# Softmax times V on one core: who writes an identity matrix, and sixteen words sent early

## The chip, the core and the metric

The kernel runs on one core of a Trainium2 chip. The core has five engines that run their own instruction streams and meet through semaphores: TensorE (PE in the profile, with its weight loads as PEld), VectorE (DVE), ScalarE (ACT), GpSimd (POOL) and SyncE (SP), which here only issues DMAs. 16 DMA engines move data between DRAM and the on-chip memory SBUF; PSUM holds what TensorE writes. The metric is the device time of one execution in microseconds (us), as the median of several. The profile shows one execution in detail.

## The reference

```python
scores: (8, 12, 1024, 1024) float32      v: (8, 12, 1024, 64) float32
scores_max = np.max(scores, axis=-1, keepdims=True)
attn = np.exp(scores - scores_max)
attn = attn / (np.sum(attn, axis=-1, keepdims=True) + 1e-8)
return np.matmul(attn, v).astype(np.float32)
```

96 heads, and for each a 1024 x 1024 matrix of scores whose rows become weights, and a product with a 1024 x 64 matrix. The scores are 403 MB, v and the result 25 MB each.

## The kernel before

**Tiling.** A pass takes four heads, as two groups `k` of two heads each; there are 24 passes, counted by `m` from 0 to 23 in one loop. In a group, a partition holds 16 rows of scores of one head (64 partitions for each head), so `s_nat` of a group is 128 x 16 x 1024 values, 8 MB. There is one such buffer for each group.

**One row.** Below, a row `r` of a group means the 128 score rows, one for each partition, that have the same place. For every two rows ScalarE writes the exponentials in half precision into one of six `p_nat` buffers (line 461). TensorE turns each row in eight blocks against the identity `ident16` into PSUM, `psT` (line 474); VectorE copies two turned rows into `pt` (line 486, the last four rows of group 1 one by one on line 482); TensorE multiplies `pt` by `vones`, v with columns of ones beside it, and sums into `psO` (line 172). The products of a row follow its transposes three rows later. For every three rows VectorE takes the reciprocals of the sums (line 150) and writes the normalised result into `out_sb`, in two halves (line 158). The maximum isn't subtracted; VectorE keeps the extremes of the reciprocals and a last check on them (lines 353 to 374) decides whether `general()`, a slow way that subtracts the maximum, runs behind the loop. With these inputs it does not.

**Order on the queues.** All transfers are issued by SyncE, in an order that `queue()` fixes. Within a pass m, when group 0 is done (`load_first`), SyncE issues v of the next pass, a store of the results of the pass before, and group 0's scores of the next pass; when group 1 is done (`last`), group 1's scores. GpSimd spreads v into `vones` (line 321) and moves `out_sb` into `done` (line 202), from which the store of a whole pass goes out in one DMA (line 226). That store carries a condition: in pass 0 there is nothing to store, and in pass 22 it is left out. The results of passes 21 and 22 go out in pass 23 from `done` and from `v_sb` (line 237, in `load_first`), and those of pass 23 in three pieces from `out_sb` (line 237, in `end`).

**The last passes.** From pass 21 on, the loads for the next pass are cut into pieces (group 0: 8, 4 and 4 rows; group 1: 4, 4, 2, 2, 2, 1 and 1), in the `Else` of two conditions. In the first 22 passes `ident16` is a permuted identity (line 82), which puts two neighbouring rows of the result into neighbouring partitions as `done` needs them; passes 22 and 23 store straight from `out_sb` and need the plain one. So in `last`, in the `Else` that passes 21 and 22 take, line 442 writes `ident16` anew, from `ident32`; that writing must wait until TensorE has turned the last row of the pass, and TensorE's next transposes wait for it. On ScalarE it stands behind `watch_v` (line 335), which reads all of v, and in front of the next pass's exponentials; the loop has no barrier, each engine goes on into the next pass as its semaphores allow.

**Declared orders.** `apart(a, b)` tells the planner that two instructions need no order between them; `send()` does this for all stores and keeps them in `stores`.

Of the kernel before, what the change touches and what calls it, by code (L numbers as in the profile page):

```python
# [26 lines left out]
def kernel(  # L27
# [6 lines left out]
    nc = tc.nc  # L34
# [5 lines left out]
    BH = B * H  # L40
# [12 lines left out]
    T = 2  # L53
    K = AHEAD // T
    W = P // T
# [12 lines left out]
    out_rows = out.rearrange("b h (j r) d -> (b h j) (r d)", j=W)  # L68
# [8 lines left out]
    ident32 = const_pool.tile([P, P], FP32, name="ident32")  # L77
    make_identity(nc, ident32)
    ident16 = const_pool.tile([P, P], FP16, name="ident16")
# [3 lines left out]
        out=ident16[:].rearrange("x (t a j) -> x t a j", t=T, a=A),  # L83
        in_=ident32[:].rearrange("x (t j a) -> x t a j", t=T, a=A),
# [38 lines left out]
    def after(a, b):  # L123

        tc.add_manual_dep(
            a.ins,
            b.ins.name,
            mybir.DependencyInfo(mybir.DependencyClass.NoSync, mybir.DependencyReason.DATA),
            reason="order",
        )  # L130
# [7 lines left out]
    def queue(dma):  # L138

        if queued:  # L140
            after(dma, queued[-1])
        queued.append(dma)
# [43 lines left out]
    def behind(a, b, reason):  # L186

        tc.add_manual_dep(
            a.ins,
            b.ins.name,  # L190
            mybir.DependencyInfo(mybir.DependencyClass.Sync, mybir.DependencyReason.DATA),
            reason=reason,
        )

    def put_by(k):

        first = None
        for t in range(T):
            for a in range(A):
                at = (t * A + a) * J  # L200
                to = (k * T + t) * J
                put = nc.gpsimd.tensor_copy(  # L202
                    out=done[to : to + J, a],
                    in_=out_bufs[k][at : at + J].rearrange("x r d -> x (r d)"),
                )
                fills.append(put)
                first = first or put
        return first

    def put_spare():  # L210

        for k in range(K):
            fills.append(
                nc.gpsimd.tensor_copy(  # L214
                    out=spare[:, k], in_=out_bufs[k][:].rearrange("x r d -> x (r d)")
                )
            )

    def of_pass(m):

        return out_runs[bass.ds(m, 1)].rearrange("o x y -> (o x) y")

    def store_before(m):

        before = (m + (PASSES - 1)) % PASSES
        send(nc.sync.dma_start(out=of_pass(before), in_=runs, cond=(before < PASSES - 3)))

    def send(dma):
        for other in stores:
            apart(dma, other)  # L230
            apart(other, dma)
        apart(dma, dma)
        stores.append(dma)
        queue(dma)

    def store_last(to, rows):
        store = nc.sync.dma_start(out=to, in_=rows)
        ends.append(store)
        send(store)

    def end():

        cut = (GROUPS - 2) * G
        for k, a, b in ((0, 0, R), (1, 0, cut), (1, cut, R)):
            n = BH - AHEAD + T * k
            store_last(
                out_rows[n * W : (n + T) * W, a * D : b * D],
                out_bufs[k][:, a:b, :].rearrange("x r d -> x (r d)"),
            )

    stores, fills, ends, norms = [], [], [], {}
    writers, users = {}, {}

    def apart(a, b, reason="stores of two heads are disjoint"):
        tc.declare_no_dep(a.ins, b.ins, across_iterations=True, reason=reason)
# [18 lines left out]
    def load(k, m, parts=(R,), r=0, **cond):  # L274
        rows_n = sc_rows[bass.ds(m, 1), k].rearrange("o x r k -> (o x) r k")
        for rows in parts:
            queue(
                nc.sync.dma_start(  # L278
                    out=s_bufs[k][:, r : r + rows, :], in_=rows_n[:, r : r + rows, :], **cond
                )  # L280
            )
            r += rows

    def load_first(m, k):


        before = queued[-1:]
        n = (m + 1) % PASSES
        with tc.If(m < PASSES - 1) as cmp:  # L289
            load_v(n)  # L290
            store_before(m)
            then = queued[-1:]
            with tc.If(m < PASSES - 3) as cmp2:
                load(0, n)
            with cmp2.Else():
                queued[:] = then
                load(0, n, (8, 4, 4))
            spread_v(k)
        with cmp.Else():
            queued[:] = before  # L300
            store_last(of_pass(PASSES - 3), runs)
            at = (PASSES - 2) * K * P
            rows = out_rows[at : at + K * P].rearrange("(k x) y -> x k y", x=P)
            store_last(rows, spare)

    def load_v(m, **cond):

        rows = v_bh.rearrange("(m x) y -> m x y", x=P)
        dma = nc.sync.dma_start(
            out=v_sb[:].rearrange("x h s l d -> x (h s l d)"),  # L310
            in_=rows[bass.ds(m, 1)].rearrange("o x y -> (o x) y"),
            **cond,
        )
        fills.append(dma)
        queue(dma)

    def spread_v(k, behind_rows=False):

        for t in range(T):
            for s in range(S):  # L320
                op = nc.gpsimd.tensor_copy(  # L321
                    out=vones[s * Q : (s + 1) * Q, k, :, t, 0:D].rearrange(
                        "i (h l) d -> i h l d", l=L
                    ),
                    in_=v_sb[(k * T + t) * Q : (k * T + t + 1) * Q, :, s],
                )
                if behind_rows and t + s == 0:
                    behind(op, norms[k], "all rows are there")
        return op

    def watch_v():


        junk = p_bufs[-1][:].rearrange("p r k -> p (r k)")
        return nc.scalar.activation(  # L335
            out=junk,
            in_=v_sb[:].rearrange("p h s l d -> p (h s l d)"),
            func=mybir.ActivationFunctionType.Abs,
            scale=1.0 / SUM_MAX,
            accum_out=seen[:, K * R + 1 : K * R + 2],  # L340
        )
# [8 lines left out]
    def fold():  # L350

        n = K * R + 1
        nc.vector.tensor_reduce(out=seen[:, 0:1], in_=seen[:, 0 : n + 1], axis=X, op=ALU.min)  # L353
        nc.vector.tensor_reduce(  # L354
            out=seen[:, n + 1 : n + 2], in_=seen[:, 1 : n + 2], axis=X, op=ALU.max
        )

    def judge(bank):

        n = K * R + 1  # L360
        part = small("part")
        nc.vector.tensor_scalar(
            out=part, in0=seen[:, n + 1 : n + 2], scalar1=1.0, scalar2=None, op0=ALU.is_le
        )
        nc.vector.scalar_tensor_tensor(  # L365
            out=right, in0=seen[:, 0:1], scalar=1.0 / SUM_MAX, in1=part, op0=ALU.is_ge, op1=ALU.mult
        )
        cell = bank[0:1, G * M : G * M + 1]
        in_line(
            nc.tensor.matmul(  # L370
                out=cell, lhsT=right[:], rhs=vones[:, 0, 0, 0, D : D + 1], start=True, stop=True
            )
        )
        nc.vector.tensor_copy(out=count[:], in_=cell)
# [45 lines left out]
    def last(m, bank):  # L420

        before = queued[-1:]
        k = K - 1
        with tc.If(m < PASSES - 1) as cmp:
            n = nc.snap(m + 1, min_val=1, max_val=PASSES - 1)
            with tc.If(m < PASSES - 2) as cmp3:
                behind(put_by(0), norms[0], "all rows are there")
                spread_v(k, True)
                watch_v()
                put_by(k)  # L430
            with cmp3.Else():
                spread = spread_v(k)
                watch = watch_v()
                gate = nc.gpsimd.tensor_copy(out=cell, in_=out_bufs[k][:, R - 1, D - 1 : D])
                for op in (watch, spread):
                    behind(gate, op, "the values have been read")
                put_spare()
            with tc.If(m < PASSES - 3) as cmp2:  # L438
                queued[:] = before
                load(k, n)  # L440
            with cmp2.Else():
                nc.scalar.copy(out=ident16[:], in_=ident32[:])  # L442
                queued[:] = before
                load(k, n, (4, 4, 2, 2, 2, 1, 1))
        with cmp.Else():
            queued[:] = before
            end()
            fold()
            judge(bank)
# [96 lines left out]
```

## Time and profile before

| what | time |
|---|---|
| median of 3 runs | 1059.33 us |
| lowest and highest | 1058.65 and 1059.74 us |
| the profiled execution | 1058.67 us |
| its span, first to last instruction | 1056.9 us |
| TensorE and its weight loads busy | 812.7 and 777.8 us |
| ScalarE busy | 750.1 us |
| VectorE busy | 705.1 us |
| GpSimd busy | 418.8 us |

How to read the profile's lines. The page gives a busy line in 40 slices as tenths, queues with packets, MB and share, and groups: line, engine, operation, out <- in, count, then busy us and mean ns of one, then idle time of the engine ahead of it and what released it. A timeline row is: start and duration in us from the span's start, engine, line, operation, out <- in with partitions x elements, count, and in brackets the idle time ahead of it and its releaser. An engine name with a q (SPq) is the engine's sequencer, for instructions that only issue or branch. A row of several instructions gives the time from the first's start to the last's end. A wait for several semaphores is put down to the one that came last by the profile; where the engine named had long been done, it was another. A row of DMA issues ends with the size and the time from issue to landing.

### The profile page before, as it was taken

The page shows a single profiled execution, that of the slowest core. Times are in us where ns is not written, and L with a number is a line of the kernel's source. Part 1 is how long each engine was busy: PE and PEld are TensorE (multiplying, and loading weights), DVE is VectorE, ACT ScalarE, POOL GpSimd, SP SyncE. Part 2 cuts the span into 40 slices and gives each one's busy share as a digit, 9 for nine tenths or more (in the row PEclk, how much of TensorE's full clock was granted, in tenths as well). Part 3 has the DMA queues.
Part 4 walks back from the last instruction along what each step waited for, and adds up shares of the span by engine and source line. Part 5 has one row for each costly group of instructions (what it writes and reads, how often), then busy time and mean ns, then how long its engine had stood idle before and what let it go on. Part 6 is the DMA issues. An engine that isn't in the chain of part 4 may idle for free.

```text
span 1056.9 us, 32833 instructions
## 1 busy us (share of the span) xinstructions
PE 812.7 (77%) x12289; PEld 777.8 (74%) x12289; DVE 705.1 (67%) x1352; ACT 750.1 (71%) x484; POOL 418.8 (40%) x571
## 2 busy tenths in 40 slices
PE   3488668887787867878678877787787876888887
PEld 3487568786787867877668776777777766878787
DVE  2377566676676756677566675676657766667788
ACT  4487578776787667876778667786687856877985
POOL 3063342633525335243362433633336334263340
PEclk9799887898998888899888898898889989789999
DMA  9999999999999999999999999999999999999997
GB/s 397 438 437 424 408 455 422 429 434 427 446 437 437 437 433 438 434 429 434 422 429 434 437 437 437 437 437 416 455 432 432 434 411 440 434 437 424 430 419 322
DMA packets 16692, 453.06 MB, mean 429 GB/s; under 512 B 1840, under 2 KB 1968, under 8 KB 2992
## 3 DMA queue, kind: packets, MB, share of 16 engines
q1 hardware_dynamic: 16688, 452.99, 99.6%
q8 instruction: 4, 0.07, 0.0%
HBM read 427.82 MB, written 27.26 MB: 431 GB/s over the span
## 4 chain that ended last, share of the span: by engine, by line
DMA 61%; PE 13%; ACT 10%; PEld 8%; DVE 5%; issue 1%; POOL 1%; SPq 0%; DVEq 0%; PEldq 0%; ACTq 0%; POOLq 0%
DMA s_nat<-in_scores_dram 61%; ACT p_nat L461 10%; PE psO L172 6%; PE psT L474 6%; PEld L474 4%; DVE pt L486 4%; PEld L172 4%; POOL vones L321 0%; DVE seen L150 0%; DVE out_sb L158 0%; POOL done L202 0%; SPq L278 0%; DVE pt L482 0%; ACTq L461 0%; PEldq L289 0%
## 5 line engine op out<-in xcount | busy, mean ns | idle before, releaser
L461 ACT ACTIVATE p_nat<-s_nat 128x2048 f16<-128x2048 f32 (+1 forms) x432 | 702.4, 1709 | 283.7 <-SPq L438 152.6
L474 PE MATMUL psT<-ident,p_nat 128*128 128x128 f16 x6144 | 517.7, 235 | 209.8 <-ACT p_nat L461 209.8
L486 DVE COPY pt<-psT 128x2048 f16<-128x2048 f16 x336 | 411.2, 1224 | 302.6 <-PE L474 137.2
L474 PEld LDWEIGHTS <-p_nat 128*128 128x128 f16 x6144 | 435.1, 120 | 222.4 <-ACT p_nat L461 222.4
L172 PE MATMUL psO<-vones,pt 128*128 128x130 f16 x6144 | 499.1, 227 | 29.1 <-DVE pt L486 13.2
L321 POOL CAST vones<-v_sb 32x512 f16<-32x512 f32 x384 | 233.2, 607 | 595.2 <-PE L474 316.8
L172 PEld LDWEIGHTS <-pt 128*128 128x128 f16 x6144 | 400.2, 101 | 51.2 <-DVE pt L486 34.0
L158 DVE TENSOR_TENSOR out_sb<-psO,seen 64x192 f32<-64x192 f32 (+1 forms) x576 | 192.0, 333 | 36.9 <-issue 13.0
L202 POOL COPY done<-out_sb 32x1024 f32<-32x1024 f32 x176 | 182.6, 1037 | 10.4
L482 DVE COPY pt<-psT 128x1024 f16<-128x1024 f16 x96 | 63.4, 681 | 1.5
L150 DVE RECIPROCAL seen<-psO 128x3 f32<-128x3 f32 (+1 forms) x288 | 49.4, 172 | 5.1 <-PE L474 1.5
L335 ACT ACTIVATE p_nat<-v_sb 128x2048 f16<-128x2048 f32 x24 | 45.6, 1900 | 0.0
L442 ACT CAST ident<-ident 128x128 f16<-128x128 f32 x2 | 0.6, 298 | 7.7 <-PE psO L172 7.7
L335 ACT ACT_TABLE_LOAD x1 | 1.3, 1283 | 5.8 <-DMA v_sb<-in_v_dram 5.8
L353 DVE TENSOR_REDUCE seen<-seen 128x1 f32<-128x34 f32 x25 | 4.7, 189 | 0.8
L335 ACT ACTIVATION_READ_ACCUMULATOR p_nat<-v_sb 128x1 f32 x24 | 4.5, 188 | 0.0
L354 DVE TENSOR_REDUCE seen<-seen 128x1 f32<-128x34 f32 x25 | 4.5, 179 | 0.0
L108 DVE MEMSET done<- 128x1024 f32 x2 | 1.8, 912 | 1.2 <-DVEq L505 1.0
L214 POOL COPY v_sb<-out_sb 128x1024 f32<-128x1024 f32 x2 | 2.0, 1040 | 0.0
L370 PE MATMUL psO<-vones,right 128*1 128x1 f16 x1 | 0.2, 164 | 1.6 <-DVE right L365 1.6
L370 PEld LDWEIGHTS <-right 128*1 128x1 f16 x1 | 0.1, 79 | 1.8 <-DVE right L365 1.8
masks.py:197 POOL MEMSET ident<- 128x128 f32 x1 | 0.2, 204 | 0.3 <-POOLq L530 0.3
(13 smaller groups left out, 2.0 us busy)
## 6 DMA issues: line engine op xcount, KB each, us to landing
v_sb<-in_v_dram SPq DMA_DIRECT2D x24, 1024.0 KB, 13.5
out_dram<-done SPq DMA_DIRECT2D x24, 1024.0 KB, 8.7
s_nat<-in_scores_dram SPq DMA_DIRECT2D x4, 4096.0 KB, 18.5
s_nat<-in_scores_dram SPq DMA_DIRECT2D x8, 2048.0 KB, 25.9
s_nat<-in_scores_dram SPq DMA_DIRECT2D x6, 1024.0 KB, 29.0
s_nat<-in_scores_dram SPq DMA_DIRECT2D x4, 512.0 KB, 26.8
out_dram<-v_sb SPq DMA_DIRECT2D x1, 1024.0 KB
s_nat<-in_scores_dram SPq DMA_DIRECT2D x43, 28.7
```

The source lines that it names most:

```text
L150: nc.vector.reciprocal(out=recip, in_=psO[:, :, D : D + 1])
L158: norm = nc.vector.tensor_tensor(out=out_bufs[k][part, g * G : g * G + rows, :], in0=psO[part, :, t * N : t * N + D], in1=recip[part].to_b ...
L172: product = nc.tensor.matmul(out=st["psO"][g][:, i * M : (i + 1) * M], lhsT=pt[:, c * P : (c + 1) * P], rhs=vones[:, k, c].rearrange("p t ...
L202: put = nc.gpsimd.tensor_copy(out=done[to : to + J, a], in_=out_bufs[k][at : at + J].rearrange("x r d -> x (r d)"),)
L321: op = nc.gpsimd.tensor_copy(out=vones[s * Q : (s + 1) * Q, k, :, t, 0:D].rearrange("i (h l) d -> i h l d", l=L), in_=v_sb[(k * T + t) * Q ...
L335: return nc.scalar.activation(out=junk, in_=v_sb[:].rearrange("p h s l d -> p (h s l d)"), func=mybir.ActivationFunctionType.Abs, scale=1. ...
L353: nc.vector.tensor_reduce(out=seen[:, 0:1], in_=seen[:, 0 : n + 1], axis=X, op=ALU.min)
L354: nc.vector.tensor_reduce(out=seen[:, n + 1 : n + 2], in_=seen[:, 1 : n + 2], axis=X, op=ALU.max)
L461: exp = nc.scalar.activation(out=p_nat[:, g : g + rows, :].rearrange("p r (x v) -> p x r v", v=Q * L), in_=s_bufs[k][:, r + g : r + g + ro ...
L474: turned = nc.tensor.transpose(out=psT[:, c * P : (c + 1) * P], in_=p_row[:, c // L, c % L, :], identity=ident16[:],)
L482: copy = nc.vector.tensor_copy(out=pt, in_=psT)
L486: copy = nc.vector.tensor_copy(out=pt2[:], in_=psT2[:])
```

## The change

```diff
+    def touch():
+
+        at = (BH - T) * W
+        dma = nc.sync.dma_start(out=out_rows[at : at + 16, 0:1], in_=ident32[0:16, 0:1])
+        for other in stores:
+            apart(dma, other)
+            apart(other, dma)
+        apart(dma, dma)
+        queue(dma)
+
@@ in load_first
             with cmp2.Else():
                 queued[:] = then
                 load(0, n, (8, 4, 4))
+                touch()
             spread_v(k)
@@ in last
             with cmp2.Else():
-                nc.scalar.copy(out=ident16[:], in_=ident32[:])
+                nc.vector.tensor_copy(out=ident16[:], in_=ident32[:])
                 queued[:] = before
                 load(k, n, (4, 4, 2, 2, 2, 1, 1))
```

The first part moves line 442 from ScalarE to VectorE, with the same operands. On VectorE it stands behind the last normalisation of the pass and in front of the next pass's copies.

The second part adds one DMA, issued by SyncE in passes 21 and 22, behind the three loads of group 0. It writes sixteen single words of the result in DRAM, one in each of sixteen partitions' runs, from `ident32`. They lie in the last two heads, whose right values the last stores of pass 23 write over them. The DMA is declared apart from the conditional store and from itself, and it is not in `stores`, so the stores of line 237 are not declared apart from it.

## The prediction

> **What bounds the kernel now.** First the page: busy time, the slices, the queues and the two lines of interest.
>
> ```profile
> span 1056.9 us, 32833 instructions
> ...
> DMA  9999999999999999999999999999999999999997
> ...
> q1 hardware_dynamic: 16688, 452.99, 99.6%
> ...
> L442 ACT CAST ident<-ident 128x128 f16<-128x128 f32 x2 | 0.6, 298 | 7.7 <-PE psO L172 7.7
> ```
>
> The 16 DMA engines move 453 MB and are full in every slice but the last. A change that moves neither bytes nor their order can only act on the last stretch, between the last loads and the end. The second thing is the moved line: two casts of 0.3 us, with 7.7 us of ScalarE idle before them, so 8.3 us of ScalarE time in all. The question is how much of it stands on the path. So next the windows of the last 80 us (columns: busy time of PE, PEld, DVE, ACT, POOL; clock; DMA share; GB/s), and ScalarE's timeline there.
>
> ```profile
> 980.00:1000.00 20.00, 15.64 (x261) 14.85 (x261) 14.13 (x27) 20.00 (x12) 9.02 (x12) 1.00 1.00 425
> ...
> 1020.00:1040.00 20.00, 19.16 (x325) 18.56 (x326) 17.16 (x31) 19.66 (x12) 4.76 (x8) 1.00 1.00 425
> ```
>
> ```profile
> 975.93 0.19 ACT L335 ACTIVATION_READ_ACCUMULATOR p_nat<-v_sb 128x1 f32 x1
> 979.19 0.30 ACT L442 CAST ident<-ident 128x128 f16<-128x128 f32 x1 [3.07 <-PE psO L172]
> 980.00 29.14 ACT L461 ACTIVATE p_nat<-s_nat 128x2048 f16<-128x2048 f32 x18 [0.51 <-PE psO L172]
> ...
> 1010.85 0.19 ACT L335 ACTIVATION_READ_ACCUMULATOR p_nat<-v_sb 128x1 f32 x1
> 1015.62 0.30 ACT L442 CAST ident<-ident 128x128 f16<-128x128 f32 x1 [4.58 <-PE psO L172]
> 1016.43 18.14 ACT L461 ACTIVATE p_nat<-s_nat 128x2048 f16<-128x2048 f32 x10 [0.51 <-PE psO L172]
> 1034.91 10.62 ACT L461 ACTIVATE p_nat<-s_nat 128x2048 f16<-128x2048 f32 x7 [0.34 <-PE psT L474]
> 1046.13 1.06 ACT L461 ACTIVATE p_nat<-s_nat 128x1024 f16<-128x1024 f32 x1 [0.59 <-PE psT L474]
> ```
>
> DMA is full (share 1.00) while ScalarE is busy 20.00 and 19.66 of 20 us and PE 19.16: three resources run level here. The two casts stand at 979.19 and 1015.62, in front of passes 22 and 23, counted from 0. An exponential of two rows takes 1.81 us (18.14 / 10).
>
> **The cast leaves ScalarE.** Without it, pass 22's first exponential starts not at 980.00 but 0.8 us behind the end of the accumulator read, as it now stands 0.8 us behind the start of the cast: 976.12 + 0.8 = 976.9, 3.1 us sooner. For pass 23 the same gives 1011.04 + 0.8 = 1011.8 or earlier, but its rows must be there. Asked by narrow windows around their issue, the loads concerned answer thus (issue to landing last): the first 8 rows, issued at 1002.14; group 1's rows 4 to 7, issued at 1006.56; its row 15, issued at 1020.36.
>
> ```profile
> s_nat<-in_scores_dram SPq DMA_DIRECT2D x1, 4096.0 KB, 13.3
> s_nat<-in_scores_dram SPq DMA_DIRECT2D x1, 2048.0 KB, 28.3
> s_nat<-in_scores_dram SPq DMA_DIRECT2D x1, 512.0 KB, 25.7
> ```
>
> ```profile
> 1002.14 0.34 SPq L278 DMA_DIRECT2D s_nat<-in_scores_dram  x1
> 1006.56 0.33 SPq L278 DMA_DIRECT2D s_nat<-in_scores_dram  x1
> 1020.36 0.33 SPq L278 DMA_DIRECT2D s_nat<-in_scores_dram  x1
> ```
>
> They land at 1015.4, 1034.9 and 1046.1. So pass 23 can start at 1015.5, only 0.9 us before 1016.43. And the exponential at 1034.91, put down to PE, stands exactly at a landing: from there ScalarE already goes at the pace of the loads and cannot be sooner.
>
> **The cast joins VectorE**, behind the last normalisation of the pass (line 158). Those rows, the copies behind them, and the PE rows:
>
> ```profile
> 981.28 0.48 DVE L158 TENSOR_TENSOR out_sb<-psO,seen 64x64 f32<-64x64 f32 x2
> 981.98 5.29 POOL L321 CAST vones<-v_sb 32x512 f16<-32x512 f32 x8 [6.16 <-DVE out_sb L158]
> ...
> 1017.72 0.47 DVE L158 TENSOR_TENSOR out_sb<-psO,seen 64x64 f32<-64x64 f32 x2
> 1018.43 1.06 PE L474 MATMUL psT<-ident,p_nat 128*128 128x128 f16 x16 [1.12 <-ACT p_nat L461]
> 1019.59 1.22 DVE L486 COPY pt<-psT 128x2048 f16<-128x2048 f16 x1 [1.39 <-PE psT L474]
> 1020.20 1.08 PE L474 MATMUL psT<-ident,p_nat 128*128 128x128 f16 x16 [0.71 <-ACT p_nat L461]
> 1021.38 1.23 DVE L486 COPY pt<-psT 128x2048 f16<-128x2048 f16 x1 [0.57 <-PE psO L172]
> 1022.00 0.64 PE L474 MATMUL psT<-ident,p_nat 128*128 128x128 f16 x8 [0.26 <-ACT p_nat L461]
> ```
>
> VectorE ends pass 22 at 1018.19. A short group of the page gives the lower end of what the cast costs:
>
> ```profile
> L354 DVE TENSOR_REDUCE seen<-seen 128x1 f32<-128x34 f32 x25 | 4.5, 179 | 0.0
> ```
>
> No row shows this cast on VectorE. Its duration lies between 0.18 us (the reductions of line 354 to 128x1) and 0.30 (ScalarE's own); I take 0.25, near the 64x64 normalisation, 0.23 each. How long after 1018.19 it issues lies between 0.1 us and the 1.4 that now pass until the copy at 1019.59; I take 0.4, nearest to the 0.51 that ScalarE spends between cast and exponential. So the identity stands at 1018.85, and the transposes of rows 0 and 1, which now start at 1018.43 when ScalarE's exponential is ready, start 0.4 us **later**. That is the new wait: behind the cast on VectorE stand the copies of pass 23, and PE waits for both. Then the gain comes: rows 0 and 1 are turned by 1019.9, rows 2 and 3 follow at once (their exponential ends at 1015.5 + 3.7 = 1019.2), not at 1020.20. The copy of rows 0 and 1 cannot start before VectorE has left the pass, about 1020.0, and ends at 1021.25, not 1020.81; the first product is at 1021.3; row 4 is turned at 1021.75, not at 1022.00, where PE now waits for ScalarE a third time. From there PE and VectorE set the pace to the end as before. **Net at 1022: 0.25 sooner; I take 0.2.**
>
> Bounds: if the cast cost nothing, PE would be sooner by up to 0.7 us (the gap before 1020.20), and not more than what is left at the landing of 1034.9:
>
> ```profile
> 1037.43 0.61 PE L474 MATMUL psT<-ident,p_nat 128*128 128x128 f16 x8
> ```
>
> These are row 4's transposes of group 1 (12 rows before the last); their exponential ends at 1034.95 + 1.8 = 1036.75. So 0.7 sooner at most. At the other end the cast issues 1.4 us late: 0.7 later.
>
> At pass 22 the same happens 36 us earlier, and there it is covered. VectorE stops for GpSimd's copies of the results:
>
> ```profile
> 990.59 0.74 DVE L158 TENSOR_TENSOR out_sb<-psO,seen 64x192 f32<-64x192 f32 x2 [2.05 <-POOL done L202]
> ```
>
> It goes on at 990.59, 2.05 us late, released by GpSimd. GpSimd's chain starts at 981.98 behind the normalisation, which does not move, so the stop ends where it did, whatever PE gained or lost before. Term 0; without that cover it would be another 0.2.
>
> **A rule against the cast's place.** GpSimd's casts of line 321 run back to back from 981.98 for 5.29 us, and likewise from 1017.57, at 0.61 us each; no row here shows a VectorE cast from SBUF to SBUF beside them. The Trainium skill's page "SBUF — State Buffer", section "Who interferes with whom", says that VectorE casts may take a port pair shared with GpSimd, and that the later of the two is blocked until the other's instruction is through. What that would do here is rival 3.
>
> **The sixteen words.** touch() issues one DMA behind group 0's loads in passes 21 and 22, two in all, on SyncE. An issue costs SyncE 0.33 us (above); behind it stands group 1's first load, and all loads of a pass lie 13 to 29 us ahead of landing in a full queue, so a third of a us is covered. If that lead were gone it would cost 2 x 0.33. In the queue, 64 bytes are nothing beside 453 MB; what a DMA costs beyond its bytes is bounded below by 0 and above by the shortest issue to landing, the last store's 2.0 us:
>
> ```profile
> out_dram<-out_sb SPq DMA_DIRECT2D x1, 128.0 KB, 2.0
> ```
>
> Two 512 KB loads of pass 22 say which end is nearer (issue, then issue to landing):
>
> ```profile
> 974.06 0.33 SPq L278 DMA_DIRECT2D s_nat<-in_scores_dram  x1
> 978.98 0.33 SPq L278 DMA_DIRECT2D s_nat<-in_scores_dram  x1
> ```
>
> ```profile
> s_nat<-in_scores_dram SPq DMA_DIRECT2D x1, 512.0 KB, 27.9
> s_nat<-in_scores_dram SPq DMA_DIRECT2D x1, 512.0 KB, 24.3
> ```
>
> They land at 1001.96 and 1003.28: 1.3 us for 0.52 MB, what 425 GB/s gives (1.23) and 0.1 more. So I take 0.1 per touch, 0.2 us on the loads of pass 23, which fits into the 0.7 that PE has in hand at 1037.43: **term 0**. One DMA more may also shift which earlier landing a later issue waits for. SyncE's waits show that such exist:
>
> ```profile
> SPq L237 <- DMA s_nat<-in_scores_dram: 20.0, 2, 18.1
> ```
>
> Stores of line 237 that were issued a load earlier would still stand behind the same loads. The last touch stands in front of loads that land by 1034.9, so the last stores, which write over its words, find it done. Term 0.
>
> **Sum.** -0.2 + 0 + 0 = -0.2 us. The profiled execution took 1058.67 with a span of 1056.9, so it should come to 1058.5; the median, 0.66 above it, to **1059.1**. Its own range, with the bounds of the cast (-0.7 to +0.7) and the 0.5 us spread of the runs, is 1058.1 to 1060.3. A measurement can tell about 0.2% from no change, 2.1 us: 1057.2 to 1061.4 counts as the same.
>
> **Rival 1, slower: the touch drains the queue.** If an engine finishes a write of a few bytes to DRAM before it goes on, each touch stops the loads for up to 2.0 us, the last store's. Two: 4.0, less the 0.7 in hand: +3.3, 1062.6. It is slower by 0.2% from 1.4 us per touch on. Against it: the 0.1 us between the 512 KB loads; but these write SBUF. The Trainium skill's page "DMA: Bandwidth & Descriptors", section "Anatomy of one DMA — SWDGE (gpsimd) path", states a fixed cost of about 2.0 us, mostly until the write is confirmed; the trace's 2.0 agrees for a lone store, the 0.1 says it overlaps in a full queue. Chance 0.15.
>
> **Rival 2, faster: the touch removes a hole.** The windows around the first store after two passes without one, issued at 1039.90:
>
> ```profile
> 1039.60:1041.60 2.00, 1.92 (x34) 1.76 (x33) 1.86 (x4) 2.00 (x2) 0.00 (x0) 1.00 1.00 416
> 1041.60:1042.80 1.20, 1.20 (x23) 1.10 (x20) 1.17 (x2) 1.06 (x2) 0.00 (x0) 1.00 1.05 290
> ```
>
> 416 GB/s falls to 290. From the landing at 1034.9 to the last at 1046.1 go 4.19 MB, 9.9 us at 425 GB/s: the last row is 1.3 us late. If the touches keep this from happening and the tail hangs on that row (its exponential starts 0.07 us behind the landing), the end gains 1.3 and pass 23's start 0.9: 1057.1. Against it:
>
> ```profile
> 1048.84 0.61 PE L474 MATMUL psT<-ident,p_nat 128*128 128x128 f16 x8
> ```
>
> The last row's exponential ends at 1047.19 and PE turns it at 1048.84: 1.65 us in hand, so the hole is hidden. Chance 0.18.
>
> **Rival 3, no change by another way: VectorE's cast waits for GpSimd**, up to one 0.61 us cast. Then PE starts pass 23 at 1019.5 and the balance at row 4 turns to +0.4: 1059.7. Chance 0.12. The forecast itself has 0.55.
>
> **Chances.** Faster 0.18 (rival 2), slower 0.15 (rival 1), same 0.67. The range 1057.2 to 1061.7 reaches to rival 2's edge and half into rival 1.
>
> **What would show it.** Right: no line 442 on ScalarE; pass 22's first exponential at about 977, pass 23's at 1015.5; VectorE's cast 0.2 to 0.9 us behind its last normalisation; VectorE's stop for GpSimd still ending near 990.6; last transposes at 1048.6. Wrong: landings of pass 23 over 1 us later (rival 1), a window at 1042 without the dip and the last store over 1 us sooner (rival 2), PE's first transposes of pass 23 after 1019.3 (rival 3); or passes before 21 that are longer, where I expect none to change.

## The result, and the profile after

The changed kernel takes 1157.7 us in the median (1155.98 to 1159.52, 6 runs) beside 1059.4 before: a ratio of 1.0929, 95% interval 1.0918 to 1.094. That is 98 us slower, far outside the predicted range. The page of the changed kernel:

```profile
span 1156.7 us, 32827 instructions
...
DMA  9998999999999899998999989999899999999997
...
q1 hardware_dynamic: 16752, 452.99, 94.3%
...
L453 DVE CAST ident<-ident 128x128 f16<-128x128 f32 x2 | 0.6, 289 | 1.1 <-issue 1.1
```

The bytes are the same, 453 MB, but the DMA engines, which were full, are full no more (94.3% for 99.6%), and the loss is spread over the whole span, not over the last passes in which the change runs. The moved cast itself is where it should be and costs 0.3 us. Next, one window from 100 to 950 us, passes 1 to some 20, of the kernel before and then of the changed one (columns as in the prediction: PE, PEld, DVE, ACT, POOL, clock, DMA share, GB/s):

```profile
100.00:950.00 850.00, 663.41 (x9940) 635.78 (x9938) 568.12 (x1087) 605.68 (x391) 353.49 (x471) 0.89 1.00 434
```

```profile
100.00:950.00 850.00, 611.76 (x9050) 587.12 (x9048) 517.58 (x990) 550.26 (x355) 320.83 (x427) 0.85 0.94 391
```

A share of 0.94 is 51 us without transfers in 850. The rate fell further, from 434 to 391, while 0.94 of 434 is 408; so the transfers that run are slower too.

SyncE's waits (waiting line, what it waited for, us in total, times, longest) of the kernel before:

```profile
SPq L278 <- ACT p_nat L461: 446.3, 49, 25.6
...
SPq L278 <- DMA s_nat<-in_scores_dram: 65.6, 26, 6.6
```

and of the changed kernel, in which line 288 is the loads' line:

```profile
SPq L288 <- DMA s_nat<-in_scores_dram: 827.5, 48, 32.3
...
SPq L288 <- ACT p_nat L472: 14.6, 1, 14.6
```

That is the reversal. Before, a load waited until ScalarE had read the rows that it overwrites. Now it waits for another load to land, 48 times, about two for each pass. SyncE's timeline of two half passes before (v on line 309, the store on 226, loads on 278; the merged row of two is group 0's load and group 1's, which starts at 582.47):

```profile
538.94 0.33 SPq L278 DMA_DIRECT2D s_nat<-in_scores_dram  x1
555.42 0.34 SPq L309 DMA_DIRECT2D v_sb<-in_v_dram  x1
556.31 0.35 SPq L226 DMA_DIRECT2D out_dram<-done  x1
562.98 19.82 SPq L278 DMA_DIRECT2D s_nat<-in_scores_dram  x2
...
606.53 0.35 SPq L278 DMA_DIRECT2D s_nat<-in_scores_dram  x1
```

The same stretch of the changed kernel, where group 1's load of the merged row starts at 646.17:

```profile
597.72 0.33 SPq L288 DMA_DIRECT2D s_nat<-in_scores_dram  x1
603.46 0.34 SPq L320 DMA_DIRECT2D v_sb<-in_v_dram  x1
604.33 0.35 SPq L226 DMA_DIRECT2D out_dram<-done  x1
619.73 26.77 SPq L288 DMA_DIRECT2D s_nat<-in_scores_dram  x2
...
668.27 26.00 SPq L288 DMA_DIRECT2D s_nat<-in_scores_dram  x2
```

A pass, from one load of group 0 to the next, takes 48.5 us for 43.6. The issue to landing of the changed kernel's loads at 597.72, 619.73 and 646.17:

```profile
s_nat<-in_scores_dram SPq DMA_DIRECT2D x1, 21.8
s_nat<-in_scores_dram SPq DMA_DIRECT2D x1, 26.2
s_nat<-in_scores_dram SPq DMA_DIRECT2D x1, 21.9
```

They land at 619.5, 645.9 and 668.1, and each time the next load goes out 0.2 to 0.3 us later: one load of scores at a time. Before, the loads at 562.98 and 582.47 took

```profile
s_nat<-in_scores_dram SPq DMA_DIRECT2D x1, 28.7
s_nat<-in_scores_dram SPq DMA_DIRECT2D x1, 28.6
```

and landed at 591.7 and 611.1; the next had been issued 9.2 and 4.6 us ahead of that. The queue never ran empty. What it costs now shows in the windows behind group 0's landing:

```profile
640.00:643.00 3.00, 1.25 (x19) 0.89 (x16) 2.38 (x8) 0.00 (x0) 0.21 (x1) 1.00 0.91 393
643.00:644.00 1.00, 0.00 (x0) 0.00 (x0) 0.00 (x0) 0.00 (x0) 0.94 (x2) 1.00 0.15 66
644.00:645.00 1.00, 0.00 (x0) 0.00 (x0) 0.00 (x0) 0.00 (x0) 0.88 (x3) 0.79 0.01 0
645.00:646.00 1.00, 0.00 (x0) 0.00 (x0) 0.00 (x0) 0.00 (x0) 0.94 (x2) 0.50 0.00 0
646.00:647.00 1.00, 0.00 (x0) 0.00 (x0) 0.00 (x0) 0.92 (x1) 0.88 (x3) 0.50 0.00 0
647.00:650.00 3.00, 1.95 (x18) 1.79 (x19) 0.02 (x1) 3.00 (x3) 2.82 (x4) 0.50 1.02 350
```

Share and rate in a short window are counted by the packets that start in it, and a packet of a whole load is 2.4 us long; so the idle time is shorter than the rows without packets look, about 3 us, and 850 us with 17.5 passes at 51 us of idle time give 2.9 for each.

**Why the loads wait.** The planner gives every DMA of SyncE in the loop one of eight completion semaphores, in turn, and a DMA waits for the last one on its semaphore to land. The Trainium skill's page "DMA: Bandwidth & Descriptors", section "Why a DMA increments its semaphore by 16 and not by 1", says what that wait is good for: the 16 engines count up one by one, so with two DMAs in flight on one semaphore a count can be reached before the first has landed whole. The trace agrees with such a wait: 0.2 to 0.3 us from each landing to the next issue. The turn, by the semaphore numbers that the traces give for each DMA (counted from 0 to 7 here):

```
                                 before         changed
v, store                         0, 1           0, 1
group 0, whole load (m < 21)     2              2
group 0, pieces (m = 21, 22)     2 3 4          2 3 4, the words 5
group 1, whole load (m < 21)     5              2
group 1, pieces                  5 6 7 0 1 2 3  2 3 4 5 6 7 0
stores of pass 23                0 1, 5 6 7     0 1, 2 3 4
```

Where two branches meet, the planner goes on from the one that is further along the circle of eight; this rule is inferred from the turns of the kernels shown here, and all of them fit it. Before, the passes' branch ended with 5 next and pass 23's branch, two stores long, with 2 next: it goes on with 5. With the words it is 6 against 2, half a circle apart either way, and the planner takes 2. So group 1's whole load, in a branch that does not hold the words, gets group 0's semaphore.

### The profile page after: what moved, and what is told of

Its sections match the earlier page's. It is cut to its first block, busy times and chain, and to the rows that moved or that the text cites. A ratio compares the mean times of both kernels' runs of the same rounds, so it can differ in the third digit from the quotient of the medians.

```text
span 1156.7 us, 32827 instructions
## 1 busy us (share of the span) xinstructions
PE 828.3 (72%) x12289; PEld 795.0 (69%) x12289; DVE 705.7 (61%) x1354; ACT 749.6 (65%) x482; POOL 418.7 (36%) x571
## 3 DMA queue, kind: packets, MB, share of 16 engines
q1 hardware_dynamic: 16752, 452.99, 94.3%
## 5 line engine op out<-in xcount | busy, mean ns | idle before, releaser
L485 PE MATMUL psT<-ident,p_nat 128*128 128x128 f16 x6144 | 528.8, 239 | 298.3 <-ACT p_nat L472 298.3
L485 PEld LDWEIGHTS <-p_nat 128*128 128x128 f16 x6144 | 445.4, 121 | 310.2 <-ACT p_nat L472 310.2
L172 PE MATMUL psO<-vones,pt 128*128 128x130 f16 x6144 | 506.6, 229 | 24.7 <-DVE pt L493 10.7
L172 PEld LDWEIGHTS <-pt 128*128 128x128 f16 x6144 | 407.2, 102 | 45.8 <-DVE pt L497 28.1
```

The source lines that it names most:

```text
L172: product = nc.tensor.matmul(out=st["psO"][g][:, i * M : (i + 1) * M], lhsT=pt[:, c * P : (c + 1) * P], rhs=vones[:, k, c].rearrange("p t ...
L485: turned = nc.tensor.transpose(out=psT[:, c * P : (c + 1) * P], in_=p_row[:, c // L, c % L, :], identity=ident16[:],)
```

## The experiments

Theory S is the one above. Rival T blames the sixteen words, rival V VectorE's identity. The first four runs are a table of two parts, each with and without the shared semaphore.

**The identity alone.**

```diff
-                nc.scalar.copy(out=ident16[:], in_=ident32[:])
+                nc.vector.tensor_copy(out=ident16[:], in_=ident32[:])
```

> Edit: the kernel before with line 442 alone moved to VectorE; no sixteen words. Theory S (the added DMA shifts the turn of completion semaphores, so that group 1's whole load of every pass gets the semaphore of group 0's load, and each waits for the other's landing): no effect, 1059 us, or up to 0.7 us less or more from the identity itself. Rival T (the sixteen words themselves, their write or SyncE's handling of them, cost the time): 1059. Rival V (VectorE's identity puts a wait on TensorE or VectorE into every pass): 1157.

1059.6 us; ratio 0.9998, interval 0.9989 to 1.0007. Rival V falls, and the identity's effect is below what can be measured. How its parts came out is told below.

**The words alone**: touch() as in the change, line 442 as before.

> Edit: the kernel before with the sixteen words alone; the identity stays on ScalarE. Theory S: group 1's load shares its semaphore with group 0's, 1157 us, the DMA share about 94%. Rival T: 1157. Rival V: 1059.

1154.2 us; ratio 1.0903, 1.0886 to 1.092. The loss comes with the words, and with the wait:

```profile
SPq L288 <- DMA s_nat<-in_scores_dram: 822.0, 48, 32.4
```

S and T both said so; the next two part them. The 3.5 us by which this is less than the whole change were not followed up.

**The whole change, with other semaphores.**

```diff
-            store_last(rows, spare)
+            for k in range(K):
+                store_last(rows[:, k : k + 1], spare[:, k : k + 1])
```

Pass 23's branch then has three DMAs, the planner meets 6 against 3 and goes on with 6.

> Edit: the changed kernel, both parts in it, with the store of pass 22's results in pass 23 issued as two DMAs, one for each group, so that the turn of semaphores comes out otherwise and group 1's load no longer shares group 0's. Theory S: 1059 us, SyncE's wait for landings ahead of group 1's whole loads gone, DMA share above 99%; perhaps 0.3 us less than before. Rivals T and V: 1157, as all that they blame is still there.

1058.9 us; ratio 0.9997, 0.9988 to 1.0006. One store cut in two, in the last pass, brings back all 98 us with both parts of the change in place. SyncE's waits and the window from 100 to 950 of this kernel:

```profile
SPq L288 <- ACT p_nat L473: 444.1, 48, 25.4
...
SPq L288 <- DMA s_nat<-in_scores_dram: 76.9, 29, 7.6
```

```profile
100.00:950.00 850.00, 665.13 (x9982) 637.10 (x9981) 570.74 (x1093) 605.54 (x390) 355.50 (x472) 0.89 1.00 434
```

The reversal is undone and the queue is full. T falls.

**Neither part of the change, with the shared semaphore.**

```diff
-                load(0, n, (8, 4, 4))
+                load(0, n, (8, 4, 2, 2))
```

> Edit: the kernel before, without either part of the change; only group 0's pieces in passes 21 and 22 are 8, 4, 2 and 2 rows instead of 8, 4 and 4, which is as many DMAs in that branch as with the sixteen words. Theory S: the same shared semaphore, 1157 us, with SyncE waiting some 24 us for group 0's landing ahead of each whole load of group 1. Rivals T and V: 1059.

1157.3 us; ratio 1.0918, 1.0896 to 1.0941. A fourth DMA in that branch does it without the words too; here it is a piece of a load in two passes. The waits:

```profile
SPq L278 <- DMA s_nat<-in_scores_dram: 823.3, 50, 32.4
```

**Where in the pass it costs.** Two waits stand in each pass: group 1's load behind group 0's landing, with nothing else queued, and group 0's behind group 1's, where v and the store are queued. The next three kernels are the changed one with whole loads cut into two halves, so that a wait ends half a load earlier. First group 0's:

```diff
-                load(0, n)
+                load(0, n, (R // 2, R // 2))
```

> Edit: the changed kernel with group 0's whole load of passes 0 to 20 cut into two halves of 8 rows, on the semaphores of which group 1's whole load shares only the first half's. Theory S with its price in the hole behind group 0's load (group 1's load is issued only when group 0's has landed, when nothing else is queued; the trace shows the DMA engines idle for some 3 us there in each pass): the wait now ends with the first half, about 10 us of loads ahead of the end of the queue, the hole is gone, and only the wait of group 0 for group 1's landing is left, which v and the store cover for 5 us: 1060 to 1090 us. Rival P (sharing a semaphore costs by the waits or by longer packets, wherever in the pass it stands): 1130 to 1157.

1078.4 us; ratio 1.0167, 1.0126 to 1.0208. 79 of the 98 us are gone by the median (its four runs lie between 1073.8 and 1082.3 us), with SyncE still waiting 517 us for landings. Its waits and window:

```profile
SPq L288 <- DMA s_nat<-in_scores_dram: 517.4, 48, 23.1
```

```profile
100.00:950.00 850.00, 643.43 (x9761) 619.92 (x9760) 556.92 (x1069) 594.86 (x384) 345.31 (x459) 0.89 1.00 424
```

The idle time is gone (1.00); 424 GB/s for 434, in a run of 1082.0 us, is most of what is left of the loss. Now group 1's load in halves, group 0's whole, by the same edit of `load(k, n)` in `last`:

> Edit: the changed kernel with group 1's whole load cut into two halves instead; the first half shares group 0's semaphore. Theory S with its price behind group 0's load: group 1's first half still waits for the whole of group 0's load, the hole stays, and only the covered wait of group 0 is shortened: 1120 to 1157 us. Rival P: half the waits are gone, so about half the loss, near 1110, as in the kernel with group 0's halves.

1158.8 us; ratio 1.0937, 1.0919 to 1.0955: nothing gained. Rival P, for which it does not matter where a wait stands, wanted 1110. The window still has the hole:

```profile
100.00:950.00 850.00, 571.69 (x8969) 547.38 (x8967) 512.31 (x983) 546.98 (x352) 319.25 (x423) 0.85 0.95 391
```

Both in halves:

> Edit: the changed kernel with both whole loads cut into halves; each half shares a semaphore with the half of the other group in the same place, so every load still waits for a landing, but one half-load before the queue runs empty. Theory S: 1059 us within 3 us. Rival P: 1157, as every semaphore is still shared.

1064.0 us; ratio 1.0046, 1.003 to 1.0063. Each load shares its semaphore and waits, 759 us in all, and nearly nothing is lost: the wait ends while another half of 10 us is queued. P falls for good. But 4.5 us are more than the 3 that were allowed. Between 100 and 950 us this kernel moves 433 GB/s; its loss lies later, in one window, behind a v that in pass 22 is issued at 1005.13 and not at 998.49 as before:

```profile
1000.00:1010.00 10.00, 9.33 (x156) 8.71 (x154) 8.98 (x20) 6.48 (x6) 0.00 (x0) 1.00 0.72 272
```

```profile
1005.13 0.33 SPq L320 DMA_DIRECT2D v_sb<-in_v_dram  x1
```

It has semaphore 0, which the last one-row piece of group 1 now has too, and is issued when that piece has landed. The test of that is the same kernel with the store cut in two as above, which moves the whole turn:

> Edit: the kernel with both whole loads in halves, and with the store of pass 22's results issued as two DMAs, as in the third run, so that no half shares a semaphore with one of the other group. Theory S: what the kernel with both halves still lost, 4.5 us, stands in its pass 22, where v is issued 6 us later than before, right behind the landing of the last one-row load, and the DMA engines run at 272 GB/s from 1000 to 1010; with other semaphores v is issued in time again and the time is 1059 within 1.5 us. Rival H (more DMAs, or a load in halves, cost the 4.5 us by themselves): 1064.

1060.7 us; ratio 1.001, 1.0 to 1.0019. That is 1.7 from 1059, where 1.5 were allowed, and 0.8 from the kernel before in the same session (1059.95). The window and the issue are mended, and 3.3 of the 4.5 us; the rest, about 1 us by the medians, may be what more DMAs cost, at the edge of what can be told:

```profile
1000.00:1010.00 10.00, 9.34 (x156) 8.71 (x154) 8.99 (x20) 8.70 (x8) 1.95 (x4) 1.00 1.05 444
```

```profile
998.03 0.33 SPq L321 DMA_DIRECT2D v_sb<-in_v_dram  x1
```

No kernel of these is measurably faster than the one before.

## Why the prediction was wrong

**The step that failed** is the last one on the sixteen words: "One DMA more may also shift which earlier landing a later issue waits for. SyncE's waits show that such exist", and then only "Stores of line 237 that were issued a load earlier would still stand behind the same loads", term 0. The mechanism was named and its reach was not: I looked at the stores of line 237 alone, and wrote of the earlier passes "I expect none to change". The shift is fixed when the program is built and holds for all passes, also in branches without the words. The term is not 0 but 98 us, nearly all of it in passes 0 to 20: two waits a pass, of which the one behind group 0's load leaves the queue empty for 2.9 us; ending that wait half a load earlier brought back 79 us of the 98 (group 0's halves). With both groups in halves some 3 us were left in pass 22, in v's wait for the last one-row piece (the last two runs).

The prediction's own rows spoke of the danger. It called a change of bytes or order the only way to act outside the last stretch; that premise failed as well, as the queue moves the same 453 MB with its loads in the same order, and what has moved is the time at which they are issued. And it hid SyncE's issue behind loads that are "13 to 29 us ahead of landing in a full queue". That lead is what the cover rests on; it asked what 0.33 us would cost without it, and not what would take the lead itself away: a wait of one load for the other's landing, of which the view of SyncE's waits had 26 already.

**Rival 1** forecast the right side by another way and is refuted: with both touches in place and other semaphores the time is that of before (0.9997), where rival 1 asked for 3.3 us more.

**The bytes of the touch**, taken as 0.1 us each and hidden: borne out by the same run. In its trace the 2 MB loads on either side of a touch land 4.89 and 4.91 us apart, and the neighbouring ones without a touch between them 4.82 to 4.90.

**The identity**, a term of -0.2 between -0.7 and +0.7: not contradicted, as the time is the same within 0.1%, but that is too coarse to tell -0.2 from 0. (The range worked out from these bounds, 1058.1 to 1060.3, starts from 1059.33 at its lower end and from 1059.1 at its upper; from 1059.33 the upper is 1060.5. It changes nothing here.) The kernel with it alone shows the steps, ScalarE first, then VectorE, then PE:

```profile
976.12 29.27 ACT L461 ACTIVATE p_nat<-s_nat 128x2048 f16<-128x2048 f32 x18
...
1015.58 18.34 ACT L461 ACTIVATE p_nat<-s_nat 128x2048 f16<-128x2048 f32 x10 [5.78 <-PE psO L172]
```

```profile
991.47 0.74 DVE L158 TENSOR_TENSOR out_sb<-psO,seen 64x192 f32<-64x192 f32 x2 [1.02 <-POOL done L202]
...
1018.60 0.47 DVE L158 TENSOR_TENSOR out_sb<-psO,seen 64x64 f32<-64x64 f32 x2
1019.57 0.25 DVE L442 CAST ident<-ident 128x128 f16<-128x128 f32 x1 [0.49 <-issue]
```

```profile
1019.96 1.95 PE L474 MATMUL psT<-ident,p_nat 128*128 128x128 f16 x32 [1.77 <-DVE ident L442]
1022.49 0.62 PE L172 MATMUL psO<-vones,pt 128*128 128x130 f16 x8 [0.58 <-POOL vones L321]
1022.95 0.61 PE L474 MATMUL psT<-ident,p_nat 128*128 128x128 f16 x8
```

The exponentials of passes 22 and 23 start at 976.1 and 1015.6 (976.9 and 1015.5 forecast), the first with none of the forecast's 0.8 us behind the read, the second held by its rows' landing. VectorE's stop for GpSimd is still there in pass 22, 0.9 us later than before. Ahead of pass 23 the cast takes 0.25 us and issues 0.50 us behind the last normalisation; ahead of pass 22 it took 0.34 us, above the 0.30 that was set as its upper bound. PE starts 0.89 us behind that normalisation, not 0.24, then turns four rows without a stop, and reaches row 4 at 3.88 us behind it, where it was 3.81: nothing won or lost, where 0.2 won was forecast. A new wait, for GpSimd's v, took 0.58 us there; the prediction did not have it.

**Rival 3** fits that no better. Its sign, PE's first transposes after 1019.3, is there by the number (1019.96), but in this run VectorE ended pass 22 at 1019.07 and not at 1018.19, and behind the last normalisation PE started after 0.89 us, where the sign asks for over 1.1. No VectorE cast stood still for a whole GpSimd cast of 0.61 us. Whether part of the 0.49 us ahead of it was such a wait, as the Trainium skill's page "SBUF — State Buffer", section "Who interferes with whom", has it, these rows can't tell.

**Rival 2** was right that the dip can shrink and wrong that this pays. The dip exists without the words too (the identity alone, around its store issued at 1039.98), and is smaller with them (the whole change with other semaphores, second store issued at 1039.71):

```profile
1041.70:1042.90 1.20, 1.11 (x20) 1.09 (x20) 1.03 (x5) 1.05 (x2) 0.00 (x0) 1.00 1.04 249
```

```profile
1041.00:1042.20 1.20, 1.20 (x25) 1.20 (x22) 1.17 (x2) 1.08 (x1) 0.00 (x0) 1.00 1.03 369
```

```profile
1042.29 4.12 ACT L473 ACTIVATE p_nat<-s_nat 128x1024 f16<-128x1024 f32 x4 [0.21 <-PE psT L486]
```

In the latter ScalarE does the last four rows without a stop and ends at 1046.41, 0.8 us sooner than before (1047.19), and the time is the same: the dip was hidden, as forecast. Whether the words or the earlier issue of the stores made it smaller wasn't tried.

**Open**: why transfers were slower as well as absent. By the pages' queue rows (99.6% of 1056.9 us, 94.3% of 1156.7) the packets took 38 us more in all, and the idle time grew by 62. From 100 to 950 us a 64 KB packet of the scores took 2.48 us in the mean for 2.42 before, and an 8 KB packet of v and the stores 0.37 us for 0.31; with both groups in halves it was 0.31 again. Open too is why group 1's halves gained nothing while, with group 0's halved already, they gained 14 us (1078.4 to 1064.0). The two waits do not add up; these runs say which one holds most of the loss, not how they act together.

## What to carry to other kernels

A DMA costs more than its bytes and its issue: where completion semaphores are handed out in turn, it moves those of every DMA behind it, in branches too that never run it, and two long loads on one semaphore run one after the other. So after adding, cutting or removing any DMA, look at SyncE's waits of a pass that the change does not touch: a load must wait for its buffer's reader, not for another load. A wait for a landing cost little here where another 10 us of loads were queued behind it: cutting the loads in halves bought back 94 of 98 us without undoing the wait. Having something queued is not always enough: with group 0's halves alone, where v and the store filled the other wait, there were still 14 us for group 1's halves to bring back.

## What was not expected of the hardware

The empty queue costs more than its 2.9 us a pass: idle time makes some 51 of the 850 us, but the rate falls by 10%, where 6% is idle. And TensorE's granted clock falls: its last matmul before the empty stretch ends at 641.7 us and its next starts at 648.05; in the windows above the clock is 1.00 until 644, 0.79 for a microsecond and 0.50 from 645 on, and it is still 0.50 when the work comes back. This goes with TensorE's pause and not with the empty queue, as the kernel before has it too, with the queue full; there TensorE stops at 566.4 us and starts again at 569.6:

```profile
568.00:569.00 1.00, 0.00 (x0) 0.00 (x0) 0.00 (x0) 1.00 (x1) 0.00 (x0) 0.87 1.00 426
569.00:570.00 1.00, 0.41 (x4) 0.41 (x5) 0.00 (x0) 1.00 (x2) 0.00 (x0) 0.50 1.97 844
```

Over the span of the changed kernel TensorE was granted 0.854 for 0.897, and its busy time rose from 812.7 to 828.3 us for the same matmuls; no run here shows whether that cost any time.
